# Sixteen first-stage weight blocks split ahead of time and kept as halves in DRAM, in a decoder layer on one core

## The chip, the cores and the metric

The kernel runs on one core of a Trainium2 chip. The metric is the device time of one execution in microseconds. Three runs of the kernel before took 1757.22, 1754.88 and 1751.27 us; the median is 1754.88.

## The reference, cut to what matters

One layer of a decoder trunk for 512 prompt tokens and 64 sample tokens (NT = 576), width 1024, all in float32:

```python
z = rmsnorm(x) @ w_in                     # q, k, v, su, sv, gate_a, gate_b
h = sigmoid(g_a) * (attention @ w_branch_a) + sigmoid(g_b) * (gmlp @ w_branch_b)
x1 = x + h @ w_out
xb = rmsnorm(x1)
sc = (xb @ peer_w_q) . sub_keys           # two halves of 128 keys, 8 heads
best, pos = top_k(...)                    # 16 experts of 128 x 128, for each head
w = softmax(best) * gelu(peer_u[idx] . xb)
x2 = x1 + sum(w * peer_v[idx])
x3 = x2 + sigmoid(rmsnorm(x2) @ w_ple_gate) * (p @ w_ple)
```

The change touches the product with `peer_u`. For 384 of the tokens (NB) the kernel doesn't gather the chosen experts: it computes gelu(xb @ peer_u) for all 16384 experts in 128 blocks (stage 1) and multiplies each by a mask matrix G that holds the gates and zeros, before the product with `peer_v` (stage 2). The other 192 tokens gather their rows.

## The kernel before, in words

**Weights in two halves.** TensorE multiplies float32 in a rounded form (fp32r). To keep the precision, every operand is cut in two: `hi` is the rounded copy, `lo` is what is left. `split` (L65 to L67) makes hi on ACT (L66) and lo on DVE (L67). A product takes three matmuls for each 128 x 128 piece: hi with hi, hi with lo, lo with hi (`tform`, L82). `load_block` (L69 to L76) loads a 128 x 1024 block of weights from DRAM on the SP queue (L71) into `w_raw`, of which there are 4 buffers, and splits it at high priority into `w_hi` and `w_lo`, 3 buffers each.

**Order of the work.** The program is written as one stream. A scheduler orders the instructions of each engine by data and priority; work of high priority goes ahead. The stages by time in the profile:

- to about 252 us: w_in, attention, gated unit, a part of the per-layer embedding (`ple`);
- about 255 to 312 us: the branch products, 8 blocks `w_br` (L512 to L526). A block makes two products (branch a and b), each of 24 matmuls over 256 and 320 token columns. Branch a goes to PSUM tiles `mm`, branch b to `sc`. DVE takes each of the four results out of PSUM (L518, into the gates `c_...`), adds the pair (L521, `t`) and splits the sum (`c<-t,c`, L67);
- about 312 to 362 us: the output product, 8 blocks `w_out`;
- about 380 to 496 us: `peer_wq`, key scores with `sk`, and the first top-k on DVE;
- from 496.6 us: stage 1. `stage1()` (L795) takes one block of `peer_uT` at a time: load, split, 24 matmuls over 384 tokens, gelu on ACT. Twenty of the first forty activations go to DRAM (`ad`, L812, on the SP queue) and come back later. Beside it DVE does the rest of the retrieval (`retrieve`, which ends for each tile of 128 tokens in its tables `e`, L691);
- when a tile's tables are there, `make_ew` (L815) turns them on TensorE (`pt<-c_ident,e`, L818), and `build_g` makes 16 tokens of the mask at a time: one-hot rows `oa` and `ob` on DVE and ACT (L843 to L852), one matmul each token (L855), a copy, and a store to `gd` (L857);
- 869.5 us: the first matmul of stage 2 (L983, `oacc`). From there the remaining blocks of `peer_uT` go beside `peer_v` to the tail.

**What sets the order around the change.** `for ti in range(3)` runs the retrieval of three tiles and puts stage-1 blocks between its steps; `S1_TOPK = (4, 9, 13)` and `S1_PRE = 33` say how many blocks the program has written by when. The scheduler moves them from there: a block comes as early as its weights are ready.

**Queues.** SP issues nearly all loads and stores in one order. POOL issues gathers and a few small loads.

Of the kernel before, what the change touches and what calls it, by code (L numbers as in the profile page):

```python
# [7 lines left out]
F32 = mybir.dt.float32  # L8
F32R = mybir.dt.float32r
# [8 lines left out]
P = 128  # L18
D = 1024
NT = 576  # L20
NB = 384
KC = 8
# [15 lines left out]
RING = 44  # L38
NXP = 24
S1_PRE = 33  # L40
TILES = [(512, 64), (0, 128), (128, 128), (256, 128), (384, 128)]
HALVES = (slice(0, 256), slice(256, 576))
EPS = 1e-6
# [4 lines left out]
def tile_decoder_step(ctx: ExitStack, tc: tile.TileContext, a, o):  # L48
    nc = tc.nc
    V, A, T, G, S = nc.vector, nc.scalar, nc.tensor, nc.gpsimd, nc.sync  # L50

    def pool(stack, name, bufs, side="left", **kw):
        return stack.enter_context(tc.tile_pool(name=name, bufs=bufs, side=side, reuse_waits="tile", **kw))

    const = pool(ctx, "const", 1)
    wp = pool(ctx, "wp", 2)
    dr = ctx.enter_context(tc.tile_pool(name="dr", bufs=1, space=DRAM))
# [7 lines left out]
    def split(src, hi, lo):  # L65
        A.activation(hi, src, AF.Copy)  # L66
        V.tensor_sub(lo, src, hi.bitcast(F32))  # L67

    def load_block(src, shape=(P, KC, P), urgent=True):  # L69
        raw = wp.tile(list(shape), F32, name="w_raw", bufs=4)  # L70
        S.dma_start(raw, src)  # L71
        hi = wp.tile(list(shape), F32R, name="w_hi", bufs=3)
        lo = wp.tile(list(shape), F32R, name="w_lo", bufs=3)
        with tc.high_priority(offset=1000 if urgent else 0):
            split(raw, hi, lo)
        return hi, lo  # L76

    def tform(ps, w, x, wk=0, nk=KC):
        n, i = 3 * nk, 0
        for k in range(nk):  # L80
            for wi, xi in ((0, 0), (0, 1), (1, 0)):
                mark_pe[0] = T.matmul(ps, lhsT=w[wi][:, wk + k, :], rhs=x[xi][k], start=i == 0,  # L82
                                   stop=i == n - 1)
                i += 1
# [7 lines left out]
    def mm():  # L92
        return psM.tile([P, 512], F32, name="mm")
# [6 lines left out]
    x1d = dr.tile([KC, P, NB], F32, name="x1d")  # L100
    pld = dr.tile([NT, D], F32, name="pld")
    ad = dr.tile([NSP, P, NB], F32, name="ad")
    gd = dr.tile([NJ // JB, P, NB // TB, JB, TB], F32, name="gd")

    psBs = ExitStack()
# [7 lines left out]
    def f4(dt=F32):  # L113
        return c4.tile([P, 4, NT], dt, name="c4")
# [4 lines left out]
    def f8(mk, *args):  # L119
        t = [mk(*args), mk(*args)]  # L120
        return [t[k // 4][:, k % 4, :] for k in range(KC)]

    def tt():
        return e1.tile([P, NT], F32, name="t", bufs=3)

    def bank(tag):
        return psB.tile([P, 512], F32, name=tag)

    def joint(w, x, out, wk=0, nk=KC, bk=mm):
        for cols in HALVES:  # L130
            ps = bk()[:, :cols.stop - cols.start]
            tform(ps, w, [[xi[k][:, cols] for k in range(nk)] for xi in x], wk, nk)
            out(ps, cols)
# [13 lines left out]
    def rstd_cols(tot, rs):  # L147
        ps = bank("sc")
        for c0, r in TILES:
            for p0 in range(0, P, r):  # L150
# [314 lines left out]
    def ple(tiles):  # L465
        wl_ = [load_block(a["w_ple"][k], (P, D)) for k in range(2)]
        for c0, r in tiles:
            pt = e1.tile([P, 2, P], F32, name="pw", bufs=3)
            S.dma_start(pt[:, :, :r], a["pT"][:, :, c0:c0 + r])
            ph, pl = (e1.tile([P, 2, P], F32R, name="pw", bufs=3) for _ in range(2))  # L470
            split(pt[:, :, :r], ph[:, :, :r], pl[:, :, :r])
            for hh in range(2):
                ps = bank("pv")
                i = 0
                for k in range(2):
                    for xi, wi in ((ph, 0), (ph, 1), (pl, 0)):
                        T.matmul(ps[:r], lhsT=xi[:, k, :r], rhs=wl_[k][wi][:, hh * 512:(hh + 1) * 512],  # L477
                                 start=i == 0, stop=i == 5)
                        i += 1
                st = e1.tile([P, 512], F32, name="st")  # L480
                A.activation(st[:r], ps[:r], AF.Copy)
                S.dma_start(pld[c0:c0 + r, hh * 512:(hh + 1) * 512], st[:r])
# [5 lines left out]
    for i in range(24):  # L488
# [4 lines left out]
        else:  # L493
            c, br = divmod(i - 8, 2)
# [13 lines left out]
        split(suT[:, g, :], mh[:, g, :], ml[:, g, :])  # L508
    e2s.close()
    ple(TILES[:3])  # L510
    ahl = [[t[:, g, :] for g in range(4)] for t in (ah, al)]
    mhl = [[t[:, g, :] for g in range(4)] for t in (mh, ml)]  # L512
    hs = ([], [])
    for c in range(KC):
        w = load_block(a["w_br"][c])
        for i, (x, k0_) in enumerate(((ahl, 0), (mhl, 4))):
            sg = sgs[2 * c + i]
            joint(w, x, lambda ps, cols: V.tensor_tensor(sg[:, cols], sg[:, cols], ps, op=ALU.mult), k0_, 4,  # L518
                  (mm, lambda: bank("sc"))[i])
        ga = tt()  # L520
        V.tensor_tensor(ga, sgs[2 * c], sgs[2 * c + 1], op=ALU.add)  # L521
        if c % 4 == 0:
            h4 = [f4(F32R), f4(F32R)]
        for h, t in zip(hs, h4):
            h.append(t[:, c % 4, :])
        split(ga, hs[0][c], hs[1][c])  # L526

    gp = pool(ctx, "gp", 2)
    rows = ExitStack()
    rowp = pool(rows, "rowp", 5)  # L530

    def row(shape=(P, D), dt=F32):
        return rowp.tile(list(shape), dt, name="row")

    x1 = f8(f4)
    xg = (f8(x4), f8(x4))
    tot, add = sumsq()
    for c in range(KC):
        w = load_block(a["w_out"][c])
        xc = tt()  # L540
        S.dma_start(xc, a["xT"][c])
        joint(w, hs, lambda ps, cols: V.tensor_tensor(x1[c][:, cols], ps, xc[:, cols], op=ALU.add))
        S.dma_start(x1d[c], x1[c][:, P:512])
        gcol = vecs[:, 8 + c:9 + c]
        A.activation(xg[0][c], x1[c], AF.Copy, scale=gcol)
        V.scalar_tensor_tensor(xg[1][c], x1[c], gcol, xg[0][c].bitcast(F32), op0=ALU.mult, op1=ALU.subtract)
        if c:
            add(c - 1, x1[c - 1])
    add(KC - 1, x1[KC - 1])
    ple(TILES[3:])  # L550

    tilesA = TILES[:2]
    accs, xrs, ixs, gts = [], [], [], []
# [209 lines left out]
    for i in range(16):  # L763
        h, c = i // 4 + i % 2 * 4, i // 2 % 2
        w = load_block(a["peer_wq"][2 * h + c])
# [17 lines left out]
    def pay(x):  # L783
        credit[0] += x
        n = int(credit[0])
        credit[0] -= n
        gather(n, mark_pe[0])
# [7 lines left out]
    def stage1():  # L795
        nonlocal j1, nlive
        j = j1
        j1 += 1
        w = load_block(a["peer_uT"][j])
        ps = (mm() if j % 2 or phase[0] > 1 else bank("pv"))[:, :NB]  # L800
        tform(ps, w, xb)
        if j in SPILL:
            act = held_x[-1][:, sorted(SPILL).index(j) % 6, :]
        else:
            n = nlive % RING
            nlive += 1
            act = held_x[n // 6][:, n % 6, :] if n < NXP - 6 else (
                acp[0][:, n - NXP + 6, :] if n < RING - 6 else held_x[-1][:, n - RING + 6, :])
        A.activation(act, ps, AF.Gelu_apprx_tanh)  # L809
        acts[j] = act  # L810
        if j in SPILL:
            S.dma_start(ad[sorted(SPILL).index(j)], act)  # L812
        pay(GP[phase[0]])
# [47 lines left out]
    for ti in range(3):  # L861
        for _ in retrieve(ti, ti < 2):
            if len(acts) < S1_TOPK[ti]:
                stage1()
        if ti == 0:
            steps.append(gather_steps())
        while len(acts) < S1_TOPK[ti]:
            stage1()
    phase[0] = 1
    rest_t = [retrieve(ti, False) for ti in (3, 4)]  # L870
    for tb in range(NB // TB):
# [9 lines left out]
        if tb < TBK:  # L881
            goal = S1_TOPK[2] + (tb + 1) * (S1_PRE - S1_TOPK[2]) // TBK
        else:
            goal = S1_PRE + (tb - TBK + 1) * (NSP + RING - 1 - S1_END - S1_PRE) // (NB // TB - TBK)
        while len(acts) < goal:
# [32 lines left out]
    def tail_turn(xn3, r, xh, xl):  # L918
        for hh in range(2):
            ps = mm()[:, :4 * r].rearrange("p (k t) -> p k t", k=4)  # L920
            for k in range(4):
                T.transpose(out=ps[:, k, :], in_=xn3[:r, (hh * 4 + k) * P:(hh * 4 + k + 1) * P],
                            identity=ident[:r, :r])
            ks = slice(hh * 4, hh * 4 + 4)
            A.activation(xh[:, ks, :r], ps, AF.Copy)
            V.tensor_sub(xl[:, ks, :r], ps, xh[:, ks, :r].bitcast(F32))
# [30 lines left out]
    def gathered(ti):  # L957
# [16 lines left out]
        tail_turn(xn3, r, xh, xh[:, :, NS:] if r == NS else xl)  # L974
        return x2, xh, xl, xn3, r, TILES[ti][0]

# [71 lines left out]
    for k in range(3, KC):  # L1048
        raw = wp.tile([P, D], F32, name="w_raw", bufs=4)
# [20 lines left out]
    for t, (x2, xn3, ss) in enumerate(xs):  # L1070
        xhl = xp.tile([P, 2, KC, P], F32R, name="x4")
        xh, xl = xhl[:, 0], xhl[:, 1]
        tail_turn(xn3, P, xh, xl)
        tails.append((x2, xh, xl, xn3, P, TILES[2 + t][0]))
        if t == 0:
# [105 lines left out]
```

## Time and profile before

| what | value |
|---|---|
| median of 3 runs | 1754.88 us |
| the profiled execution | 1754.17 us |
| its span (first to last instruction) | 1752.4 us |
| mean granted TensorE clock | 0.997 |
| ACT busy | 856.7 us (49%) |
| POOL busy | 525.0 us (30%) |
| DMA, mean over the span | 457.07 MB, 261 GB/s |

The busy times are of one execution, on the one core. PE is TensorE, PEld its weight loads, DVE VectorE, ACT ScalarE. `x24` behind an instruction is how many alike stand in that row. Duration of neighbours can overlap by a pipeline's depth, so the time from one start to the next (a slot) may be shorter than a duration. In a table of windows each row gives the window, its length, the busy time of PE, PEld, DVE, ACT and POOL with the number of instructions, the granted clock (PEclk, 1.00 is full), the busy share of the 16 DMA engines and the GB/s.

### The profile page before, as it was taken

How to read it: one execution, taken by the hardware profiler on the slowest of the kernel's cores; microseconds unless marked ns; L12 is line 12 of the kernel's file. 1: busy time of each engine (PE TensorE's matmuls, PEld its weight loads, DVE VectorE, ACT ScalarE, POOL GpSimd, SP SyncE). 2: the span in 40 equal slices, each digit the busy share in tenths (PEclk: the TensorE clock that was granted, in tenths of full speed). 3: DMA queues.
4: the chain of work that ended last, by engine and by line, in shares of the span. 5: the costliest groups of instructions: out<-in, count | busy, mean ns of one | idle time of the engine just before them, and what ended most of it. 6: DMA issues, size and time to landing. Idle time of an engine off the chain costs nothing.

```text
span 1752.4 us, 27777 instructions
## 1 busy us (share of the span) xinstructions
PE 1723.8 (98%) x10102; PEld 1565.3 (89%) x10102; DVE 1435.9 (82%) x2880; ACT 856.7 (49%) x1519; POOL 525.0 (30%) x390
## 2 busy tenths in 40 slices
PE   8999999999999899999999999999999999999998
PEld 7988999999999899999888888899998999887777
DVE  6364666559999999999798899998888888999854
ACT  6565453343344798999733333333333333333442
POOL 0000000000002112444245555454544544566300
PEclk9999999999999999999999999999999999999999
DMA  7211233443236578999999999999999999999742
GB/s 241 92 61 49 73 112 118 155 142 97 82 100 242 192 229 253 361 354 358 347 375 363 377 395 410 402 410 363 361 338 361 359 340 323 337 383 375 291 132 78
DMA packets 176601, 457.07 MB, mean 261 GB/s; under 512 B 15568, under 2 KB 77008, under 8 KB 174416
## 3 DMA queue, kind: packets, MB, share of 16 engines
q1 hardware_dynamic: 120880, 253.22, 40.8%
q0 software_dynamic: 55584, 202.07, 31.0%
q8 instruction: 79, 1.29, 0.3%
q14 instruction: 58, 0.48, 0.1%
HBM read 420.18 MB, written 35.78 MB: 260 GB/s over the span
## 4 chain that ended last, share of the span: by engine, by line
PE 86%; DVE 7%; DMA 3%; ACT 2%; issue 1%; POOL 1%; SPq 0%; DVEq 0%; POOLq 0%; ACTq 0%
PE mm L82 38%; PE oacc L983 29%; PE pv L82 5%; PE sc L855 2%; PE pt L855 2%; PE oacc L942 2%; DVE w_lo L67 2%; PE sc L82 1%; DMA row<-peer_v,idx 1%; PE pv L477 1%; ACT w_hi L66 1%; PE pv L334 1%; PE sc L610 1%; POOL row L740 1%; DVE row L752 0%
## 5 line engine op out<-in xcount | busy, mean ns | idle before, releaser
L66 ACT ACTIVATE w_hi<-w_raw 128x1024 fp32r<-128x1024 f32 x325 | 344.0, 1059 | 369.7 <-PE mm L82 279.4
L740 POOL DMA_INDIRECT row<-peer_u,idx x192 | 262.6, 1368 | 846.3 <-DVE pos L661 498.4
L67 DVE TENSOR_TENSOR w_lo<-w_raw,w_hi 128x1024 fp32r<-128x1024 f32 x325 | 396.5, 1221 | 79.9 <-ACT w_hi L66 78.8
L82 PE MATMUL mm<-xd,w_hi 128*128 128x384 f32 x1552 | 404.6, 339 | 0.5 <-ACT w_hi L66 0.5
L740 POOL DMA_INDIRECT row<-peer_v,idx x192 | 260.9, 1359 | 237.2 <-DVE acc L759 212.8
L82 PE MATMUL mm<-x,w_hi 128*128 128x320 f32 (+1 forms) x1504 | 307.0, 298 | 0.5 <-ACT qp L769 0.5
L82 PEld LDWEIGHTS mm<-xd,w_hi 128*128 128x128 f32 x1552 | 280.2, 188 | 6.0 <-ACT w_hi L66 0.8
L82 PE MATMUL mm<-xd,w_lo 128*128 128x384 f32 x776 | 263.1, 339 | 1.5 <-DVE w_lo L67 1.5
L759 DVE SCALAR_TENSOR_TENSOR acc<-row,wts,acc 128x1024 f32<-128x1024 f32 x192 | 245.7, 1280 | 3.0 <-DMA row<-peer_v,idx 2.6
L82 PEld LDWEIGHTS mm<-x,w_hi 128*128 128x128 f32 x1504 | 240.1, 188 | 6.1 <-issue 3.9
L983 PE MATMUL oacc<-w_hi,wh 128*128 128x512 f32 x768 | 242.5, 396 | 1.8 <-ACT wh L66 1.8
L983 PE MATMUL oacc<-w_hi,wl 128*128 128x512 f32 x768 | 242.1, 397 | 0.6 <-DVE wl L67 0.6
L983 PE MATMUL oacc<-w_lo,wh 128*128 128x512 f32 x768 | 241.9, 396 | 0.0
L752 DVE SCALAR_TENSOR_TENSOR row<-row,xr 128x1024 f32<-128x1024 f32 x192 | 231.5, 1219 | 11.2 <-DMA row<-peer_u,idx 11.2
L82 PE MATMUL mm<-x,w_lo 128*128 128x320 f32 (+1 forms) x752 | 222.0, 295 | 0.0
L983 PEld LDWEIGHTS oacc<-w_hi,wl 128*128 128x128 f32 x768 | 144.8, 189 | 35.9 <-DVE wl L67 1.0
L983 PEld LDWEIGHTS oacc<-w_lo,wh 128*128 128x128 f32 x768 | 144.6, 188 | 34.5
L983 PEld LDWEIGHTS oacc<-w_hi,wh 128*128 128x128 f32 x768 | 143.8, 188 | 31.7 <-ACT wh L66 2.1
L82 PEld LDWEIGHTS mm<-xd,w_lo 128*128 128x128 f32 x776 | 146.2, 188 | 2.2 <-DVE w_lo L67 2.1
L82 PEld LDWEIGHTS mm<-x,w_lo 128*128 128x128 f32 x752 | 141.2, 188 | 3.5 <-issue 3.2
L82 PE MATMUL pv<-xd,w_hi 128*128 128x384 f32 x496 | 137.1, 349 | 0.7 <-ACT x L809 0.7
L66 ACT ACTIVATE wh<-x 128x384 fp32r<-128x384 f32 x66 | 34.7, 526 | 164.4 <-PE oacc L983 153.0
(329 smaller groups left out, 2348.3 us busy)
## 6 DMA issues: line engine op xcount, KB each, us to landing
w_raw<-peer_uT SPq DMA_DIRECT2D x128, 512.0 KB
w_raw<-peer_v SPq DMA_DIRECT2D x128, 512.0 KB
gd<-gs SPq DMA_DIRECT2D x24, 1024.0 KB
gs<-gd SPq DMA_DIRECT2D x15, 1536.0 KB
w_raw<-w_in SPq DMA_DIRECT2D x30, 512.0 KB
w_raw<-peer_wq SPq DMA_DIRECT2D x16, 512.0 KB
w_raw<-w_br SPq DMA_DIRECT2D x8, 512.0 KB
w_raw<-w_out SPq DMA_DIRECT2D x8, 512.0 KB
```

The lines of the kernel that those rows point to most:

```text
L66: A.activation(hi, src, AF.Copy)
L67: V.tensor_sub(lo, src, hi.bitcast(F32))
L82: mark_pe[0] = T.matmul(ps, lhsT=w[wi][:, wk + k, :], rhs=x[xi][k], start=i == 0, stop=i == n - 1)
L334: ins = T.matmul(pvs[pr, :], lhsT=vt[:, t0 + j, pr], rhs=pT, start=j == 0, stop=j == nj - 1)
L477: T.matmul(ps[:r], lhsT=xi[:, k, :r], rhs=wl_[k][wi][:, hh * 512:(hh + 1) * 512], start=i == 0, stop=i == 5)
L610: T.matmul(ps[:, b * P:(b + 1) * P], lhsT=qp[:, b * P:(b + 1) * P], rhs=sk, start=True, stop=True)
L740: ins = G.indirect_dma_start(out=row_, out_offset=None, in_=table, in_offset=bass.IndirectOffsetOnAxis(ap=ix, axis=0))
L752: V.scalar_tensor_tensor(row_, row_, 1.0, xrs[ti], op0=ALU.mult, op1=ALU.mult, accum_out=dots[:, s:s + 1])
L759: V.scalar_tensor_tensor(accs[ti], row_, wts[:, s:s + 1], accs[ti], op0=ALU.mult, op1=ALU.add)
L855: T.matmul(pt[:, t * P:(t + 1) * P], lhsT=oa[:, t, :], rhs=ob[:, t, :], start=True, stop=True)
L942: T.matmul(p[:r, :hs.stop - hs.start], lhsT=xi[:, k, :r], rhs=w[k][wi][:, hs], start=k == 0 and xi is xh and wi == 0, stop=k == KC - 1 and ...
L983: mark_pe[0] = T.matmul(oacc[t][hh], lhsT=wi[:, ts], rhs=vi[:, hh * 512:(hh + 1) * 512], start=j == 0 and last == 0 and vi is vh, stop=j = ...
```

## The change

Sixteen blocks of `peer_uT` (`NPRE`) are split early. `halves(j)` is written after each load of `w_br` (j = 0 to 7) and of `w_out` (j = 8 to 15): it loads the raw block on the SP queue, splits it at ordinary priority into `hi` and `lo` in a pool `prep` with 3 buffers of each kind, and stores both to a DRAM tensor `ud` over POOL's queue, 512 KB each. In stage 1 the first 16 blocks load `w_hi` and `w_lo` from `ud`, so no ACT or DVE work is left there for them; blocks 16 to 127 go as before. The pools `gp` and `rowp` open later, where `prep` has closed.

```diff
+NPRE = 16
...
+    ud = dr.tile([NPRE, 2, P, KC * P], F32, name="ud")
...
     ple(TILES[:3])
+    pres = ExitStack()
+    prep = pool(pres, "prep", 3, "right")
+
+    def halves(j):
+        raw = prep.tile([P, KC * P], F32, name="raw")
+        S.dma_start(raw, a["peer_uT"][j].rearrange("p k n -> p (k n)"))
+        hl = [prep.tile([P, KC * P], F32R, name=nm) for nm in ("hi", "lo")]
+        split(raw, *hl)
+        for i in range(2):
+            G.dma_start(ud[j, i], hl[i].bitcast(F32))
...
         w = load_block(a["w_br"][c])
+        halves(c)
...
         w = load_block(a["w_out"][c])
+        halves(KC + c)
...
     ple(TILES[3:])
+
+    pres.close()
+    gp = pool(ctx, "gp", 2)
...
-        w = load_block(a["peer_uT"][j])
+        if j < NPRE:
+            w = [wp.tile([P, KC, P], F32R, name=nm, bufs=3) for nm in ("w_hi", "w_lo")]
+            for i in range(2):
+                S.dma_start(w[i].rearrange("p k n -> p (k n)").bitcast(F32), ud[j, i])
+        else:
+            w = load_block(a["peer_uT"][j])
```

In the changed code the lines stand lower: the split is L67 and L68 there, the load L72, the branch's DVE work L532 and L535, `e` L707, `make_ew` L839.

**DVE, branch products.** The rows below are DVE's work of before where block 5 of `w_br` ends and block 6 is taken out (`c_2107` holds the gates of blocks 4 and 5, `c_2397` those of 6 and 7; `t` is the sum of a pair; `w_lo` is the split of a weight block two blocks ahead):

```order
L518 TENSOR_TENSOR c_2107<-c_2107,sc 128x256
L518 TENSOR_TENSOR c_2107<-c_2107,sc 128x320
L521 TENSOR_TENSOR t<-c_2107 128x576
L67 TENSOR_TENSOR w_lo<-w_raw,w_hi 128x1024
L67 TENSOR_TENSOR c_3105<-t,c_3104 128x576
L518 TENSOR_TENSOR c_2397<-c_2397,mm 128x256
L518 TENSOR_TENSOR c_2397<-c_2397,mm 128x320
```

The same place now, with two of the early splits (`lo<-raw,hi`, of the fifteenth and sixteenth block; `c_2108` and `c_2398` are the gates):

```order
L532 TENSOR_TENSOR c_2108<-c_2108,sc 128x256
L68 TENSOR_TENSOR lo<-raw,hi 128x1024
L532 TENSOR_TENSOR c_2108<-c_2108,sc 128x320
L68 TENSOR_TENSOR lo<-raw,hi 128x1024
L68 TENSOR_TENSOR w_lo<-w_raw,w_hi 128x1024
L535 TENSOR_TENSOR t<-c_2108 128x576
L532 TENSOR_TENSOR c_2398<-c_2398,mm 128x256
L532 TENSOR_TENSOR c_2398<-c_2398,mm 128x320
```

All sixteen `lo` stand in DVE's order before the output product: one to three ahead of the branch products, four to six in block 0 of `w_br`, and two in each of the blocks 1 to 5, between the taking-out of `mm` and that of the second `sc`. The eight that were written beside `w_out` have moved forward too. The last rows of POOL's order here are the stores of hi 13, hi 14, lo 13, lo 14, hi 15, hi 16, lo 15, lo 16.

**SP, opening of stage 1.** SP's order of before (`sk` are the key tables, `ad` the stores of activations):

```order
L71 DMA w_raw<-peer_uT 128x1024 x2
L767 DMA sk<-sub_kT 128x128
L71 DMA w_raw<-peer_uT 128x1024 x4
L812 DMA ad<-x_5602 128x384
L71 DMA w_raw<-peer_uT 128x1024 x3
```

And now:

```order
L72 DMA w_raw<-peer_uT 128x1024
L818 DMA w_hi<-ud 128x1024
L818 DMA w_lo<-ud 128x1024
L818 DMA w_hi<-ud 128x1024
L783 DMA sk<-sub_kT 128x128
L818 DMA w_lo<-ud 128x1024
```

The raw loads of blocks 16 to 19 come first now, since their buffers are free, and the pairs from `ud` follow as `w_hi` and `w_lo` come free.

**DVE, the third tile's tables.** DVE's order of before at the end of the third tile's retrieval (`row,dots` is a row product of the gathered tokens, `l` and `pr` are steps to `e`):

```order
L752 SCALAR_TENSOR_TENSOR row,dots<-row,xr 128x1024
L719 TENSOR_TENSOR ge<-sp,cst 128x2048
L67 TENSOR_TENSOR w_lo<-w_raw,w_hi 128x1024
L680 TENSOR_TENSOR pr<-ge,ib 128x2048
L67 TENSOR_TENSOR w_lo<-w_raw,w_hi 128x1024
L686 TENSOR_TENSOR l_6342<-pr 128x1024
```

And now:

```order
L735 TENSOR_TENSOR ge<-sp,cst 128x2048
L677 MAX_INDEX pos<-best,c_6602 128x8
L696 TENSOR_TENSOR pr<-ge,ib 128x2048
L674 MATCH_REPLACE c_6608<-best,cand 128x50
L702 TENSOR_TENSOR l_6449<-pr 128x1024
L675 MAX best<-c_6608 128x8
```

Ahead of the third `e` stood 21 splits of `peer_uT` blocks, two of them before the last key scores; one is left, that of block 16, and 4 row products stand there instead of 5. On TensorE the third tile's `make_ew` stands behind 360 stage-1 matmuls (15 blocks) where it stood behind 480 (20 blocks), and the first matmul of stage 2 behind 62.0 blocks instead of 62.8.

More of the change, by code (lines that the diff above doesn't have):

```diff
@@ L526, in tile_decoder_step @@
         split(ga, hs[0][c], hs[1][c])
[L528 to L533, printed above, removed]
     x1 = f8(f4)
@@ L550, in tile_decoder_step, with row @@
     ple(TILES[3:])
+    pres.close()
+    gp = pool(ctx, "gp", 2)
+    rows = ExitStack()
+    rowp = pool(rows, "rowp", 5)
+    def row(shape=(P, D), dt=F32):
+        return rowp.tile(list(shape), dt, name="row")
     tilesA = TILES[:2]
```

## The prediction

> **What bounds the kernel now.** I read the page first, then the table of windows, the waits of PE, the chain and the timelines.
>
> ```profile
> span 1752.4 us, 27777 instructions
> PE 1723.8 (98%) x10102; PEld 1565.3 (89%) x10102; DVE 1435.9 (82%) x2880; ACT 856.7 (49%) x1519; POOL 525.0 (30%) x390
> ```
>
> PE has work or a started matmul for all but 29 us of the span. A change that leaves PE's work alone, as this one does, can only win where PE waits or runs slowly. The table of windows says where:
>
> ```profile
> core 0: us, PE busy (x) PEld busy (x) DVE busy (x) ACT busy (x) POOL busy (x), PEclk, DMA share, GB/s
> 242.00:256.00 14.00, 14.00 (x96) 12.73 (x95) 7.93 (x12) 7.74 (x14) 0.00 (x0) 1.00 0.32 114
> 256.00:276.00 20.00, 19.96 (x133) 18.55 (x132) 12.90 (x22) 10.21 (x16) 0.00 (x0) 1.00 0.57 191
> 276.00:296.00 20.00, 20.00 (x153) 20.00 (x152) 13.56 (x24) 5.26 (x6) 0.00 (x0) 1.00 0.22 79
> 296.00:306.00 10.00, 10.00 (x78) 10.00 (x78) 5.75 (x12) 2.17 (x3) 0.00 (x0) 1.00 0.33 107
> 496.60:588.50 91.90, 84.63 (x484) 82.99 (x481) 90.32 (x387) 50.12 (x65) 12.55 (x10) 0.99 0.54 185
> 588.50:680.00 91.50, 89.25 (x556) 86.19 (x557) 89.10 (x254) 82.11 (x173) 14.40 (x10) 0.97 0.73 229
> 680.00:840.00 160.00, 159.96 (x1071) 152.84 (x1069) 158.89 (x317) 149.26 (x358) 77.47 (x52) 1.00 1.00 346
> 1040.00:1080.00 40.00, 40.00 (x192) 34.67 (x191) 39.72 (x64) 14.23 (x19) 21.84 (x15) 1.00 1.02 406
> 496.60:869.50 372.90, 361.52 (x2288) 348.18 (x2285) 358.96 (x991) 305.58 (x653) 109.33 (x76) 0.99 0.82 276
> ```
>
> The change takes work out of the fifth of these rows, the opening of stage 1, where DVE is busy 90.3 of 91.9 us and PE idles 7.3. It puts that work into the first four, the branch products, where PE idles nowhere, DVE is busy 40.1 of 64 us and ACT 25.4.
>
> How much is there to win between 496.6 and 869.5 us? A block takes 24 matmuls, and a token of the mask one:
>
> ```profile
> 505.24 4.16 PE pv L82 x24
> 681.28 0.89 PE sc L855 x8
> L855 PE MATMUL sc<-ob,oa 128*128 128x128 f32 x384 | 69.0, 284 | 1.4 <-DVE ob L846 0.7 <-DVE best L659 0.7
> L855 PE MATMUL pt<-ob,oa 128*128 128x128 f32 x384 | 58.3, 280 | 0.1
> ```
>
> The first two rows are of the chain of waits, the others groups of this stretch. At PE's own pace the stretch needs 62.8 blocks x 4.16 = 261.2, 768 mask matmuls x 0.89/8 = 85.4 and some 2 us of transposes, 348.6 of its 372.9 us. The slack is 24.3 us, and no gain can exceed it. Its pieces:
>
> ```profile
> PE pt L818 <- DVE e L691: 4.8, 1, 4.8
> PE oacc L983 <- ACT wh L66: 1.8, 1, 1.8
> 560.00:600.00 40.00, 33.22 (x182) 31.67 (x181) 37.65 (x138) 22.86 (x39) 5.04 (x3) 0.91 0.46 160
> 588.49 0.48 PE L818 MATMUL pt<-c_ident,e 128*128 128x128 f32 x1 [4.81 <-DVE e L691]
> 588.16 0.27 DVE L691 TENSOR_TENSOR e<-l 128x128 f32<-128x128 bf16 x1
> ```
>
> TensorE stands at 588.49 until DVE has the third tile's `e`: 4.8 us, with another 2.5 of idle time before. The clock of 0.91 over 40 us costs up to 3.6 more after it; the wait for stage 2's first operand is 1.8. The rest, some 11 us, lies mostly in 588 to 680, where DVE is busy 89.1 of 91.5 us and the first mask groups come one by one.
>
> **The gain in stage 1.** What a split takes of DVE's time is its slot, from its start to the next:
>
> ```profile
> 517.73 1.22 DVE L67 TENSOR_TENSOR w_lo<-w_raw,w_hi 128x1024 fp32r<-128x1024 f32 x1
> 518.87 0.42 DVE L686 TENSOR_TENSOR l<-pr 128x512 bf16<-128x512 bf16 x1
> L67 DVE TENSOR_TENSOR w_lo<-w_raw,w_hi 128x1024 fp32r<-128x1024 f32 x19 | 23.1, 1217 | 0.0
> L752 DVE SCALAR_TENSOR_TENSOR row<-row,xr 128x1024 f32<-128x1024 f32 x5 | 6.1, 1216 | 1.1 <-DMA row<-peer_u,idx 1.1
> ```
>
> The slot is 518.87 - 517.73 = 1.14 us. Of the 19 splits from 496.6 to 588.5 (third row, by groups) 18 go, by the order; of the row products one of five goes behind `e`, at about the same slot. DVE reaches the third `e` 19 x 1.14 = 21.7 us sooner: at 588.2 - 21.7 = 566.5 instead of 588.2. But PE's order moved too: `make_ew` now stands behind 15 blocks, and PE gets there at 496.6 + 15 x 4.16 = 559.0, if it never waits. So PE waits 566.5 + 0.3 - 559.0 = 7.8 us, where its idle time was 7.3: the wait stays in size, and what goes is the rest. After it I take 4.3 us for the first mask groups, still paced by DVE (a replay of the new order with the median slots of the trace; ends 0 and 8), 3.0 of half clock, as now, and 0.8 of small waits. Stage 2's first wait falls to about nothing: 3.5 blocks and a mask group now cover the last mask's way through DRAM, 18.2 us, against 13.6 (2.4 blocks and a group), and the way takes:
>
> ```profile
> 854.34 6.90 DMA gd<-gs
> 861.33 6.96 DMA gs<-gd
> ```
>
> The slack after is 7.8 + 4.3 + 3.0 + 0.8 = 15.9 of 24.3, so the gain is 8.4 us (ends 3 and 14: the mask groups' 4 either way, the wait an us or two). That stage 2 begins 0.8 blocks sooner is neutral: they are done later at the same price.
>
> The pairs from `ud` are 1.05 MB for each 4.16 us, 252 GB/s, where the opening moves 185 with a share of 0.54; 406 was reached later. They wait on SP behind `ad` stores that wait for ACT, as the raw loads do now. If a pair is late in the first 15 blocks, the 7.8 us wait covers it. Uncovered, a late pair costs what it is late.
>
> **The cost in the branch products.** ACT gets 16 x 1.06 = 17 us, DVE 16 x 1.14 = 18.2:
>
> ```profile
> L66 ACT ACTIVATE w_hi<-w_raw 128x1024 fp32r<-128x1024 f32 x325 | 344.0, 1059 | 369.7 <-PE mm L82 279.4
> ```
>
> Both fit in their idle time of 24 us and more there. POOL's issues have nothing else beside them (0.00 in the rows). What does not fit is the DMA. Each block adds a load and two stores of 524 kB, 25.2 MB in all, and the order puts all sixteen before the end of the sixth branch block. With three buffers a `lo` waits until the `lo` of three blocks before is stored, and behind the waiting split on DVE stand the takings-out of PSUM for which PE waits. These are the rows:
>
> ```profile
> 241.11 0.34 SPq L71 DMA_DIRECT2D w_raw<-w_br  x1
> 297.57 0.42 DVE L518 TENSOR_TENSOR c<-c,sc 128x256 f32<-128x256 f32 x1 [0.77 <-PE sc L82]
> 299.86 0.76 DVE L521 TENSOR_TENSOR t<-c 128x576 f32<-128x576 f32 x1
> 305.64 3.17 PE mm L82 x24
> ```
>
> The first early load follows about where `w_br` 2 is issued, 241 to 242. The last split, the sixteenth, needs the thirteenth `lo` stored: the 27th of the 32 stores, with 15 raw loads before it, 42 x 0.524 = 22.0 MB. To this comes what moves there anyway: 14 x 114 + 20 x 191 + 20 x 79 + 10 x 107 kB = 8.1 MB, less one `w_out` block that now stands behind, 7.5. At 406 GB/s, the fullest row above, 29.5 MB take 72.7 us. With 2 us for the first load to land, 242 + 74.7 = 316.7. Then DVE has the split (1.14), a `w_lo` (1.14), the sum `t` (0.7 of its 0.76) and the first taking-out (0.3 of its 0.4), 3.3 us, before PE may begin `mm` of the eighth block: 320.0, where the chain has 305.64. PE loses 14.4 us, most of it already at the second half of block 6, whose bank waits behind the fifteenth split. Such waits are longer than the 4.8 us that were followed by half clock; I add 1.7 (of 0 to 3.6). The cost is 16.1.
>
> The ends: at 346 GB/s, the row of 680 to 840 us (many small packets in it), the 29.5 MB take 85.3 us and the cost is 28.7; if the raw loads begin before 242 and no half clock follows, it is some 8. I take the 406 because the new transfers are large ones, like most of that row. Nothing gives the time back: `w_out` keeps PE busy without a gap, and later stages just begin later. The load of `w_out` behind the last raws lands before its turn, since PE is late itself.
>
> The Trainium skill's "DMA: Bandwidth & Descriptors" has in "Anatomy of one DMA — SWDGE (gpsimd) path" a fit whose variable part is bytes / 436e3 us; by it the 29.5 MB would take 67.7 us, and the cost would be about 5 us less. The same page, in "Where 436 GB/s comes from", says that between HBM and SBUF the HBM side binds at about 358 GB/s; by that the cost would be nearly 10 us more, but the row with 406 over 40 us speaks against it.
>
> **The sum.** 1754.2 + 16.1 - 8.4 = 1761.9 for the profiled execution (span and 1.8 outside). This execution stood 0.7 under the median of the three runs, so 1762.6; I say 1763. A measurement of this kernel can tell about 0.3%, 5.3 us, from no change.
>
> **The rivals.**
>
> *The two sums cancel (no change, 0.23).* The transfers run faster than 406 GB/s, since they are all large. At 440 the 29.5 MB take 67.0 us, PE loses 8.7, the waits fall to the size that leaves the clock alone, and 8.4 come back: 1755. For it: the fullest row mixes in gathers. Against it: its DMA share is 1.02 at 406, no room is left. The 436 GB/s of the Trainium skill's fit, on the page "DMA: Bandwidth & Descriptors", would make this rival the likeliest.
>
> *Faster (0.20).* The early loads start before 242, in the stretch with a share of 0.32, so that the stores stay ahead of DVE until the last blocks: cost 6 to 8. And the mask groups, with four blocks more of PE work beside them, stop waiting: gain 14. 1754.9 + 7 - 14 = 1748. Its point of decision is whether PE waits in branch blocks 0 to 4. For it: PE waited nowhere there, and buffers for three blocks are in flight. Against it: 25 MB can't go through 62 us beside 8 at any rate seen.
>
> *Slower still (0.15).* Stores beside loads move no more than in the row of 680 to 840, 346 GB/s, in which `gd` is stored: cost 28.7, gain 8.4, 1775. Against it: those stores are cut in small packets, these are not. The 358 GB/s that the Trainium skill states on the same page lie near this rival.
>
> *It does not do what it says* (0.03 of the 0.15): if pairs from `ud` come late, PE waits in the first 15 blocks, beyond the 7.8 us. That decides from 2 x 524 kB in over 4.16 + 7.8/15 = 4.7 us, under 224 GB/s, and would take the gain away: 1771. The rate of 406 speaks against it.
>
> **How the numbers follow.** My own case gets 0.42, of which 0.06 ends within 0.3%. Faster is 0.20, within 0.3% is 0.23 + 0.06 = 0.29, slower is 0.36 + 0.15 = 0.51. The range goes from 1747, the faster case, to 1777, a little over the slowest, and leaves out what lies beyond either. My own case alone would be 1756 to 1770.
>
> **What would show it.** Right, if PE waits in branch blocks 5 to 7 for DVE, with a DMA share near 1 from 245 to 320 us; if `w_out` begins some 16 us late; if a wait for the third `e` stays, of 6 to 9 us; if stage 2 begins about 8 us late against 869.5, and the rest keeps its length. Wrong, if the DMA share there stays under 0.9 while PE waits (then a chain of single transfers is the cost, not the rate), or if `make_ew` does not wait, or if a stretch after stage 2's start changes its length by more than 2 us.

## The result, and the profile after

The changed kernel takes 1767.77 us (median of 6 runs, 1764.85 to 1770.07) where the kernel before takes 1751.69 (6 runs): a ratio of 1.0085, interval 1.0071 to 1.0099, by the ratio some 15 us slower. Its profiled execution took 1769.75 us with a span of 1768.0, the span of before was 1752.4: 15.6 us more. Among the experiments one execution of gain and two of bufs4 ran in a slow state, at 2093 to 2401 us with a granted clock of about 0.75 or less, and no ratio counts them. The page after:

```profile
span 1768.0 us, 27925 instructions
PE 1727.3 (98%) x10102; PEld 1569.1 (89%) x10102; DVE 1435.3 (81%) x2880; ACT 857.1 (48%) x1519; POOL 542.7 (31%) x422
```

PE has the same 10102 matmuls, and its busy time grew by 3.5 us only: the rest of the 15.6 us is waiting. The table of windows over the branch products shows where (columns as before: PE, PEld, DVE, ACT, POOL, clock, DMA share, GB/s):

```profile
242.00:256.00 14.00, 14.00 (x95) 12.65 (x94) 9.96 (x13) 10.43 (x17) 3.19 (x6) 1.00 0.87 319
256.00:276.00 20.00, 13.13 (x60) 11.14 (x60) 8.71 (x14) 8.37 (x14) 3.18 (x6) 0.74 1.03 388
276.00:296.00 20.00, 18.63 (x140) 18.21 (x140) 16.40 (x24) 9.14 (x11) 4.25 (x8) 1.00 1.01 391
296.00:306.00 10.00, 6.47 (x48) 6.10 (x47) 4.53 (x7) 4.28 (x6) 1.75 (x4) 1.00 1.03 417
306.00:330.00 24.00, 21.04 (x146) 20.71 (x146) 19.81 (x30) 8.71 (x10) 4.59 (x9) 0.93 0.96 373
242.00:306.00 64.00, 52.23 (x337) 48.11 (x335) 39.59 (x54) 32.22 (x45) 12.37 (x24) 0.92 0.99 378
```

Before, PE was busy for all but 0.04 of these 64 us and DMA moved 79 to 191 GB/s. Now the DMA engines are full (share 0.99 over 64 us, 378 GB/s; over 1.00 from 256 us on) and PE misses 12 of the 64 us. Note that DVE and ACT are busy for no more than 40 and 32 us: they don't work, they wait. The waits of PE (total, times, longest) and of ACT in this stretch name for what:

```profile
PE sc L83 <- DVE c L532: 7.4, 3, 3.5
PE pv L479 <- ACT pw L67: 6.9, 1, 6.9
PE mm L83 <- DVE c L532: 0.5, 1, 0.5
```

```profile
ACT hi L67 <- DMA raw<-peer_uT: 19.7, 9, 5.1
ACT c L67 <- DVE t L535: 8.7, 2, 4.7
ACT hi L67 <- DMA ud<-hi: 5.2, 2, 3.6
```

The early splits `hi` stand in ACT's order and wait there for their raw block, or for the store that frees their buffer: 24.9 us together. What PE needs stands behind them. The longest of PE's waits, 6.9 us, is that for `pw`, the split of a small input of the per-layer embedding that the scheduler puts among the matmuls of the first branch block. ACT's timeline there:

```profile
260.38 1.06 ACT L67 ACTIVATE hi<-raw 128x1024 fp32r<-128x1024 f32 x1 [1.59 <-DMA ud<-hi]
265.08 1.06 ACT L67 ACTIVATE hi<-raw 128x1024 fp32r<-128x1024 f32 x1 [3.63 <-DMA ud<-hi]
266.04 1.06 ACT L483 ACTIVATE st<-pv 128x512 f32<-128x512 f32 x2
268.92 0.42 ACT L67 ACTIVATE pw<-pw 128x256 fp32r<-128x256 f32 x1 [1.81 <-DMA pw<-pT]
```

Two `hi` wait for stores, then a copy `st` is late, then `pw` waits 1.81 us more for its own load. That load ends last: SP issued it at 259.3 us, and it landed at 268.9, on the full DMA; in before the same load took no more than 3.0 us. So PE would have waited nearly as long without the two late `hi`: in bufs4 `hi` waits only 0.95 us there, and PE still waits 7.2 us for `pw`. At the end of the stage it is DVE that holds PE. The chain of waits:

```profile
319.95 0.41 DVE c L532
320.36 1.14 DVE lo L68
321.50 0.40 DVE c L532
321.89 1.14 DVE lo L68
323.03 1.13 DVE w_lo L68
324.17 0.67 DVE t L535
324.84 0.34 DVE c L532
325.18 0.14 issue
325.32 3.41 PE mm L83 x24
```

This is the row of instructions shown for the change, the fifteenth and the sixteenth `lo` with the takings-out behind them. The eighth block begins at 325.32 where it began at 305.64. PE's own wait there is only 0.5 us, since it had lost 19.2 us by then.

In stage 1 the third tile's `e` does come as early as worked out, but PE is late itself by then:

```profile
587.27 0.33 PE L839 MATMUL pt<-c_ident,e 128*128 128x128 f32 x1 [1.47 <-DVE e L707]
```

```profile
PE sc L876 <- DVE ob L867: 2.5, 1, 2.5
PE pv L83 <- DMA w_lo<-ud: 2.2, 2, 1.7
PE pt L839 <- DVE e L707: 1.5, 1, 1.5
PE pv L83 <- DMA w_hi<-ud: 0.8, 2, 0.5
PE mm L83 <- DMA w_lo<-ud: 0.7, 1, 0.7
```

The wait for `e` is 1.5 us instead of 4.8, and 3.7 us of waits for pairs from `ud` stand ahead of it.

Milestones, read from PE's instructions in the two traces and in those of the experiments (us; for the kernels after the first column, the difference to before):

| what | before | after | gain | cost | thin | pace16 | bufs4 | half8 | pace8 | pace12 | top16 |
|---|---|---|---|---|---|---|---|---|---|---|---|
| last matmul of the branch products begins | 311.7 | +19.9 | 0.0 | +20.1 | +1.8 | 0.0 | +17.0 | +10.7 | +0.5 | -0.3 | 0.0 |
| stage 1 begins | 496.6 | +21.5 | +1.2 | +20.4 | +3.4 | +1.7 | +17.0 | +10.4 | +2.3 | +0.7 | +1.9 |
| stage 2 begins | 869.5 | +13.4 | -7.5 | +18.1 | -5.5 | -7.8 | +7.9 | +0.9 | -7.3 | -8.0 | -2.8 |
| its 1000th matmul begins | 1256.9 | +16.2 | -3.8 | +17.7 | -2.3 | -5.7 | +10.8 | +4.0 | -5.4 | -4.3 | +1.6 |
| span | 1752.4 | +15.6 | -4.5 | +17.3 | -3.2 | -7.0 | +10.3 | +2.7 | -6.2 | -5.2 | +3.9 |

### The profile page after: what moved, and what is told of

It is laid out like the page before. It is cut to its first block, busy times and chain, and to the rows that moved or that the text cites. A ratio compares the mean times of both kernels' runs of the same rounds, so it can differ in the third digit from the quotient of the medians.

```text
span 1768.0 us, 27925 instructions
## 1 busy us (share of the span) xinstructions
PE 1727.3 (98%) x10102; PEld 1569.1 (89%) x10102; DVE 1435.3 (81%) x2880; ACT 857.1 (48%) x1519; POOL 542.7 (31%) x422
## 4 chain that ended last, share of the span: by engine, by line
PE 72%; DVE 9%; issue 8%; DMA 5%; POOL 5%; ACT 1%; POOLq 0%; SPq 0%; DVEq 0%; ACTq 0%
PE mm L83 33%; PE oacc L1004 23%; POOL row L756 5%; PE pv L83 4%; PE sc L876 2%; PE oacc L963 2%; PE pt L876 2%; DMA row<-peer_v,idx 2%; DMA row<-peer_u,idx 2%; DVE w_lo L68 1%; DMA raw<-peer_uT 1%; PE pv L479 1%; PE sc L83 1%; ACT w_hi L67 1%; PE pv L336 1%
## 5 line engine op out<-in xcount | busy, mean ns | idle before, releaser
L67 ACT ACTIVATE w_hi<-w_raw 128x1024 fp32r<-128x1024 f32 x309 | 327.1, 1059 | 337.1 <-PE mm L83 272.3
L68 DVE TENSOR_TENSOR w_lo<-w_raw,w_hi 128x1024 fp32r<-128x1024 f32 x309 | 377.1, 1221 | 86.2 <-ACT w_hi L67 86.0
L67 ACT ACTIVATE wh<-x 128x384 fp32r<-128x384 f32 x66 | 34.7, 526 | 163.7 <-PE oacc L1004 154.8
```

## The experiments

Two theories of the loss were set against each other. **Rate**: the early blocks bring more bytes into 70 us than DMA moves. **Order**: ACT and DVE stand in their order behind early splits that wait for one transfer after another, whatever the size; buffers or places are the cause.

**gain** leaves out the early work but for one block, and keeps stage 1's new loads.

```diff
-        halves(c)
+        if c == 0:
+            halves(0)
...
-        halves(KC + c)
...
-                S.dma_start(w[i]..., ud[j, i])
+                S.dma_start(w[i]..., ud[0, i])
```

> Only block 0 is split early and stored; stage 1 loads the same stored pair for all of its first 16 blocks, so its loads and waits are those of the changed kernel while 15 of the 16 early splits and their transfers are gone (the output is not the reference's). Both theories: the branch products keep their time (the eighth begins within 2 us of 305.6), stage 2 begins 7 to 9 us sooner than before's 869.5, and the time is 1743 to 1747 us, 5 to 8 under before.

The ratio was 0.9987 (0.9977 to 0.9997), 1749.79 us beside 1752.53: some 2 us faster, under what was expected. Stage 2 begins 7.5 us sooner, as expected, yet 3.7 of it are gone by its 1000th matmul. That is the work that was moved: stage 2 begins behind 62.0 blocks instead of 62.8, and 0.8 x 4.16 = 3.3 us of blocks are done later. So the 7.5 at that point were never a gain in full.

**cost** keeps the early work and lets stage 1 split all blocks itself.

```diff
-        if j < NPRE:
+        if j < 0:
```

> All sixteen early splits and stores stay, but stage 1 loads raw blocks and splits them as before, so nothing is won back. Both theories: the branch products lose about 20 us as in the changed kernel, the rest is as before, 1771 to 1775 us.

1770.88 us, a ratio of 1.0106 (1.009 to 1.0121), about 18.6 us, just under the range that was expected. The branch products lose 20.1 us, as in the changed kernel (19.9). By the 1000th matmul of stage 2 the loss is 17.7, though stage 1 is that of before: the half clock behind the third `e` lasted 3.41 us here and 6.83 in before, and PE's wait ahead of stage 2 was 0.6 us here and 1.8 there. So single traces differ by some 2.7 us for such reasons. 17.3 of cost alone and -4.5 of gain alone make 12.8 us of span; the change has 15.6, so the two parts add up to about that.

**thin** keeps every early instruction, buffer and store, but makes the stores of blocks 1 to 15 an eighth as wide.

```diff
-            G.dma_start(ud[j, i], hl[i].bitcast(F32))
+            n = P if j else KC * P
+            G.dma_start(ud[j, i, :, :n], hl[i][:, :n].bitcast(F32))
...
-                S.dma_start(w[i]..., ud[j, i])
+                S.dma_start(w[i]..., ud[0, i])
```

> The early raw loads, splits, buffers and all 32 stores stay where they are in the order, but the stores of blocks 1 to 15 write 128 of 1024 columns, so early bytes fall from 25.2 to about 11.4 MB; stage 1 loads block 0's pair sixteen times (the output is not the reference's). Theory of the rate (DMA can't move the bytes in the time): 18.6 MB at 390 GB/s end by about 292 us, before the eighth block's turn, so the loss falls to 0 to 4 us and the time is 1744 to 1750. Theory of the order (ACT and DVE stand in order behind early splits whose transfers come one after another, whatever their size): 12 us or more of the loss stay, 1757 to 1765.

1749.0 us, a ratio of 0.9978 (0.9968 to 0.9988). The loss in the branch products falls from 19.9 to 1.8 us. The same stretch in the table of windows of this kernel:

```profile
256.00:276.00 20.00, 18.98 (x124) 17.65 (x124) 17.03 (x25) 14.20 (x21) 4.56 (x9) 1.00 0.92 314
276.00:296.00 20.00, 20.00 (x154) 20.00 (x154) 18.85 (x29) 11.99 (x15) 6.71 (x13) 1.00 0.94 333
296.00:306.00 10.00, 10.00 (x77) 10.00 (x76) 8.42 (x12) 3.43 (x4) 2.69 (x5) 1.00 0.41 134
```

All sixteen splits are over by about 305 us (292 was expected), the share falls to 0.41 from 296 us on, and PE works. The instructions of DVE, ACT and PE stand in the same order as in the changed kernel, throughout, so the places of the splits, with less than half of the early bytes, cost under 2 us: it is the bytes. The theory of the order falls in its own form.

**pace16** moves all bytes, but holds each split behind the matmuls of its own weight block. The dependence acts on the scheduler's order alone and adds no semaphore.

```diff
-        split(raw, *hl)
+        after(A.activation(hl[0], raw, AF.Copy), mark_pe[0])
+        after(V.tensor_sub(hl[1], raw, hl[0].bitcast(F32)), mark_pe[0])
...
-        halves(c)
...
         split(ga, hs[0][c], hs[1][c])
+        halves(c)
...
-        halves(KC + c)
...
         joint(w, hs, lambda ps, cols: ...)
+        halves(KC + c)
```

> As the changed kernel, but each early split is held behind the matmuls of its own weight block (by scheduling order alone), one to each of the 8 blocks of w_br and the 8 of w_out. Theory of the rate: 41 MB over 120 us are 340 GB/s, which fits; the loss falls to 0 to 5 us, the gain of about 8 in stage 1 stays, 1744 to 1750 us, faster than before. Theory of the order: ACT and DVE still wait in order for each raw block, 8 us or more of loss stay, 1752 to 1760.

1747.74 us, a ratio of 0.998 (0.9971 to 0.9989): faster than before, by some 3.5 us. Its windows over the branch and the output products:

```profile
242.00:306.00 64.00, 63.96 (x453) 61.25 (x453) 45.88 (x71) 31.94 (x45) 6.94 (x13) 1.00 0.79 281
306.00:312.00 6.00, 6.00 (x47) 6.00 (x46) 4.90 (x8) 2.36 (x4) 1.07 (x2) 1.00 0.93 332
312.00:362.00 50.00, 50.00 (x379) 49.77 (x378) 35.37 (x47) 25.38 (x31) 8.53 (x16) 1.00 1.02 398
```

The same 25.2 MB go through 120 us instead of 80, and PE loses nothing, not even in the last row where the share is 1.02. The change loses because the scheduler drew all sixteen blocks together into the branch products. The eight that were written beside the output product are only half of it: in half8 (below) the other eight alone cost 10.7 us there.

**bufs4** is the changed kernel with four buffers of each kind.

```diff
-    prep = pool(pres, "prep", 3, "right")
+    prep = pool(pres, "prep", 4, "right")
```

> The changed kernel with four buffers of each kind for the early blocks instead of three. Theory of the rate: the same bytes go through the same 70 us, the loss in the branch products stays at 18 to 22 us and the time at 1764 to 1770. Theory of the order: one more block in flight takes a good part of the waits away, the loss falls to 10 to 14 us, 1756 to 1762.

The ratio was 1.0083 (1.0067 to 1.0099), that of the change. Its profiled execution, the fastest of its runs, lost 17.0 us in the branch products, a little under the 18 that the theory of the rate gave at least. DMA there is as full as with three buffers (388 GB/s, share 1.01). More room doesn't help where the rate is used up.

**half8** is the change with only the eight blocks beside `w_br`.

```diff
-NPRE = 16
+NPRE = 8
...
-        halves(KC + c)
```

> Only the eight blocks written beside w_br, not held back; the order puts their splits before the end of the second branch block. Theory of the rate: 12.6 MB less, so the waits of blocks 4 to 7 (10.6 us) go, and what remains is the wait of the first two blocks, 6 to 10 us; half the splits gone from stage 1 give 2 to 4 back: 1756 to 1760. Theory of the order: the waits come of the splits' places, and the first two blocks keep theirs with 9 to 10: 1758 to 1761; the two differ little here, the run gives the dose.

1756.91 us, a ratio of 1.0028 (1.0019 to 1.0037), about 5 us. Half the bytes cost 10.7 us instead of 19.9, a little over the 6 to 10 that were expected. 9.3 of them are lost before the second block begins, where one wait of PE and the clock behind it make it up:

```profile
PE pv L479 <- ACT pw L67: 7.2, 1, 7.2
PE mm L83 <- ACT w_hi L67: 1.0, 1, 1.0
```

```profile
256.00:276.00 20.00, 12.78 (x63) 10.96 (x62) 8.93 (x14) 8.47 (x14) 3.18 (x6) 0.83 1.01 396
276.00:306.00 30.00, 29.00 (x219) 28.74 (x218) 24.22 (x38) 11.90 (x15) 2.13 (x4) 1.00 0.66 244
```

**pace8** and **pace12** hold back eight and twelve blocks as pace16 does, in every second and in three of four weight blocks. The edit of pace8 (pace12 has `NPRE = 12` and `c % 4 < 3` in these places):

```diff
-NPRE = 16
+NPRE = 8
...
-        halves(c)
+        if c % 2:
+            halves(c // 2)
...
-        halves(KC + c)
+        if c % 2:
+            halves(4 + c // 2)
```

> Eight blocks, held back as in pace16, one to every second weight block of w_br and w_out. No loss in the branch products. Eight splits of DVE less before the third e than in pace16 are saved, so e comes at about 575 us; make_ew stands behind 17 blocks (567 us), a wait of 6 to 9 us stays, and pairs from DRAM are late for fewer blocks than in pace16. 1746 to 1750 us; if the late pairs are what limits pace16, it is no slower than pace16 (1747.7), if DVE's splits are, it is 2 to 4 us slower.

> Twelve blocks, held back as in pace16, in three of every four weight blocks. No loss in the branch products. The gain of stage 1 was 7.8 us to stage 2's start with sixteen and 7.3 with eight, so the dose hardly matters between them: 1745 to 1749 us, within 2 us of both. If the late pairs (sixteen) and the wait for e (eight) were separate costs with a best dose between, twelve would be 2 to 4 us faster than both, 1743 to 1746.

pace8 took 1748.14 us, 0.9972 (0.996 to 0.9984), and pace12 1747.54 us, 0.9973 (0.9964 to 0.9983). The three can't be told apart; each is faster than before by 3.5 to 5 us. In pace8 no pair is late, and the wait for `e` is there instead:

```profile
PE pt L842 <- DVE e L710: 5.6, 1, 5.6
PE mm L83 <- ACT qp L788: 2.0, 2, 1.5
```

In pace16 the opening of stage 1 (500 to 600 us) has late pairs (4.2 us) and 0.9 for `e`:

```profile
PE sc L877 <- DVE ob L868: 2.5, 1, 2.5
PE mm L83 <- DMA w_lo<-ud: 2.0, 2, 1.1
PE pv L83 <- DMA w_lo<-ud: 1.9, 2, 1.3
PE pt L840 <- DVE e L708: 0.9, 1, 0.9
PE pv L83 <- DMA w_hi<-ud: 0.3, 1, 0.3
```

One wait takes the other's place, and the dose hardly matters.

**top16** is pace16 with the third `make_ew` three blocks later.

```diff
-S1_TOPK = (4, 9, 13)
+S1_TOPK = (4, 9, 16)
```

> pace16 with S1_TOPK = (4, 9, 16): make_ew of the third tile stands behind 18 blocks instead of 15. If the wait for e is what limits the gain in stage 1, it goes and 3 to 6 us are won against pace16, 1742 to 1745; if the late pairs from DRAM are the limit (6 us of waits over blocks 9 to 16), they stay, and the time is that of pace16 within 2 us, 1746 to 1750.

Neither: 1759.39 us, a ratio of 1.0045 (1.003 to 1.006), slower than before and some 11 us slower than pace16. The wait for `e` is gone and 3.8 us of late pairs stay, but the masks begin later (`make_ew` at 578.4 against 567.7 us) and wait for DVE after that:

```profile
PE sc L877 <- DVE ob L868: 5.7, 3, 4.5
```

Stage 2 begins 5 us later than in pace16, and by its 1000th matmul 7.4. So the early place of `make_ew`, with its wait, is no waste: the mask work of DVE can't begin before it. Where the other 4 us of the difference arise wasn't followed up.

## Why the prediction was right, and what in it was off

The forecast was slower, 1763 us in a range of 1747 to 1777; measured were 1767.77. The mechanism, DMA overfilled in the branch products, was right, and two terms were mis-sized, both the same way. Beside the kernel before, the forecast was 7.7 us of loss (16.1 - 8.4), and the spans differ by 15.6, about twice that. The forecast time looks nearer than it was because the six runs of before have a median of 1751.69, 3.2 us under that of the first three.

**The cost, 16.1 us: 19.9 by the end of the branch products.** The chain at the end was right, and the bytes nearly: the sixteenth split began at 321.8 us where the sum has 316.7, and the eighth block at 325.32 where it has 320.0. What was mis-sized is the rate, and with it 14.4 -> 19.7 us. Two rows of after:

```profile
242.00:322.00 80.00, 65.76 (x426) 61.56 (x425) 51.73 (x73) 39.29 (x52) 16.11 (x31) 0.91 0.99 385
256.00:322.00 66.00, 51.77 (x333) 48.91 (x333) 41.77 (x61) 28.86 (x37) 12.92 (x25) 0.90 1.02 399
```

The sum took 406 GB/s from the start; the mean was 385. The sum's own 29.5 MB at 385 take 76.6 us, so 242 + 2 + 76.6 + 3.3 = 323.9, and some more bytes than counted make the rest (80 us at 385 are 30.8 MB). Stores between the loads took little, since from 256 us on the rate was 399. What was missing is the start, 319 GB/s at a share of 0.87 over the first 14 us: SP issued three raw loads at 241.1, and the next three only at 249.4, when the first splits (on ACT from 247.1) had freed buffers.

The Trainium skill's "DMA: Bandwidth & Descriptors" gives 436 in its fit ("Anatomy of one DMA — SWDGE (gpsimd) path") and about 358 for the HBM side ("Where 436 GB/s comes from"); the trace lies between, with 399 from 256 to 322 us here and 398 in the output products of pace16.

**The place of the waits.** The prediction put them in blocks 5 to 7 for DVE, counted from 0, most of it at block 6. The table of PE's instructions has 9.3 us lost before block 1, 5.5 more in block 4, 4.3 in block 5 and 0.7 at block 7. It had overlooked what else loads there: the small load of `pw` came late on the full DMA, and PE needs it in block 0. ACT's order was overlooked too, where `hi` waits. I take it that the total comes out the same wherever the waits lie, since the chain of splits behind the DMA holds the eighth block; no run tests that by itself. Counted at PE, 14.8 us are waits, where the sum has 14.4, and the half clock cost up to 4.6 us, where it has 1.7. By the trace's clock records the clock was halved from 265.0 to 275.3 us, 4.4 of them in the wait for `pw`, and from 309.4 to 312.8.

**The gain, 8.4 us: about 5 in this trace.** Between the beginning of stage 1 and the 1000th matmul of stage 2 the loss falls from 21.5 to 16.2, by 5.3. In cost, with stage 1 as before, it falls by 2.7, so not all of the 5.3 is shown to come of the change; the ratios of cost and of the change differ by 0.0021, 3.7 us. The forecast for `e` held: 566.5 us worked out, and in gain DVE begins it at 566.0, though stage 1 begins 1.2 us later there. The end of stage 2's first wait held too; its first matmul, at 882.85, is in this row:

```profile
880.00:900.00 20.00, 20.00 (x104) 18.33 (x103) 15.32 (x22) 8.08 (x13) 1.94 (x2) 1.00 1.01 389
```

The row of before around its own first matmul, at 869.5, has the wait and the half clock in it:

```profile
860.00:880.00 20.00, 18.17 (x88) 15.85 (x87) 11.92 (x17) 8.75 (x18) 1.01 (x1) 0.91 0.92 326
```

What did not come is the gain at the masks: the sum let them keep 4.3 of about 11 us of slack, which it placed mostly in 588 to 680 us. From 600 to 680 us, with `make_ew` at nearly the same time in both traces, PE's busy time rises only from 77.8 to 78.9 us. DVE is nearly as full as it was (79.8, now 77.6 of 80). And about half of that slack was no waiting. In the row of 680 to 840 us that the prediction shows, PE is busy for 159.96 of 160 us, and 500 of its 1071 matmuls are of the mask:

```profile
680.00:840.00 160.00, 73.90 (x500) 1.00 1.00 346
```

At the sum's own paces these are 500 x 0.89/8 + 571 x 4.16/24 = 154.6 us, 5.4 less than they took. In after it is 4.8 (471 of the mask and 593 others in the same window). So the sum's paces were too fast for this stretch, and a change that only ends waits can't win that time. (The trace has two mask matmuls for each token, 768 for 384 tokens; the prediction's words say one, its sum counts all 768.) That the late pairs would be covered by the wait for `e` held in size: 3.7 us of late pairs and 1.5 of `e` stand where 7.8 of `e` were foreseen.

**A term that was not there.** Some 1 to 2 us go between the output product and the first key score, in after (21.8 against 19.9), gain, thin and the paced kernels, but not in cost, bufs4 and half8. It is not one cause. In pace16, pace8, pace12 and top16 PE waits there 1.3 to 1.5 us for `qp` from ACT. In after, gain and thin PE doesn't wait; there the clock is halved for 3.41 us. The same window of after and of cost:

```profile
382.00:400.00 18.00, 18.00 (x102) 14.13 (x101) 7.38 (x10) 10.23 (x17) 0.00 (x0) 0.91 0.24 85
```

```profile
382.00:400.00 18.00, 18.00 (x112) 14.34 (x112) 8.73 (x12) 11.02 (x19) 0.00 (x0) 1.00 0.31 99
```

The later opening of `rowp` is in all of these kernels, also in the three without the loss, so it can't be the cause by itself. Why the clock fell there is not shown.

**Its own signs.** A DMA share near 1 came (0.99 from 242 to 322 us). `w_out` began 19.9 us late instead of some 16. Two signs did not come: the wait for the third `e` was 1.5 us and not 6 to 9, and stage 2 began 13.4 us late and not about 8. One sign against it came, though barely: from there to the end the time grew by 2.2 us, where more than 2 was to speak against it; the 0.8 blocks that are now done behind stage 2's start (3.3 us) are in it.

**The chances.** Of the rivals, "slower still" came nearest in size, with a mean of 385 between 406 and 346; its reason, stores beside loads, did not hold, as the 399 shows. For "the two sums cancel", more than 406 came only for short stretches (417 from 296 to 306 us). "Faster" failed at its own point: PE waits in block 0 already. "It does not do what it says" had its condition in 224 GB/s; the opening of stage 1 moved more (293 from 518.2 to 587.3 us), and the pairs were late by 3.7 us in all.

## What to carry to other kernels

Work that is moved under another stage has to fit its DMA, not only its idle engines: add the bytes, divide by a rate measured over a whole stretch of such transfers, its slow start included, and compare with the time up to the instruction that closes the stage. A scheduler that fills idle slots will draw such work together as early as its data allow; a dependence that only orders, one block to each step, kept the same bytes from costing anything here. And what a point in the middle gains is to be counted with the work that was moved past it.

## What the runs showed of the hardware

The clock did not follow the length of the waits. In before, 4.8 us of waiting went with a clock of 0.91 over 40 us, and the 1.8 us before stage 2 with 0.91 over 20. In after, the waits of 3.5 us and less from 276 to 306 us left the clock at 1.00, and those from 306 to 330, of 2.5 us and less, brought it to 0.93. One and the same wait of 2.5 us for the first `ob` was followed by half clock in gain and not in pace16, and from 391.3 us on in after the clock was halved with no wait at all. The Trainium skill's "TensorE: Matmul & The Clock Gate", "Part 1: The HAM clock gate", speaks of a free-running window of about 3.4 us. The traces agree with that: in the clock records of all eleven, the stretches between two changes of the clock are multiples of 3.41 us (in after, half clock for 10.24 us from 265.0, and for 3.41 from 309.4, from 391.3 and from 592.7). What in a window halves the clock no run here shows.
